# A three-pass fp32 trunk on one core: half changes that keep the last pair's weights, first residuals in a pool of their own, casts queued behind a copy, and the final norm's loads one step ahead

## The chip, the cores and the metric

One of the eight cores of a Trainium2 chip runs the whole program: TensorE (PE) multiplies, VectorE (DVE) and ScalarE (ACT) do everything elementwise, SyncE (SP) issues the loads and stores. The time is the device time of one execution in microseconds, given as the median of the runs shown.

## What is computed

The reference is one layer of a trunk on x of shape (1, 2048, 1024) in float32, cut here to what matters:

```python
h = rmsnorm(x, norm_mix_w)
proj = jnp.einsum("btd,dc->btc", h, w_in)            # 5648 columns
u_b, u_c, u_h, z, xbc, dt_raw = jnp.split(proj, SPLITS, axis=-1)
y_a = u_b * causal_dwconv(u_c * u_h, conv_w)         # gated short convolution
y_b = ssd_mixer(z, xbc, dt_raw, ...)                 # Mamba-2 scan in chunks of 64, 16 heads
x = x + jnp.einsum("btc,cd->btd", jnp.concatenate([y_a, y_b], axis=-1), w_out)
h = rmsnorm(x, norm_mlp_w)
hid = jnp.square(jax.nn.relu(jnp.einsum("btd,df->btf", h, w_up)))   # 4096 wide
x = x + jnp.einsum("btf,fd->btd", hid, w_down)
return rmsnorm(x, final_norm_w)
```

## The kernel before

**Products.** Every float32 operand is split into a high part (a cast, made on ScalarE: `L103` for weights, `L319` for activations) and a low part (operand minus high part, a subtraction on VectorE: `L104` and `L320`). A product is three matmuls, high by high (`L269`), high by low (`L270`), low by high (`L271`). The input projection, the MLP's up projection and its down projection use a Strassen-like scheme with seven products in place of eight (`Seven.chain`): for a pair of weight blocks and two blocks of 512 positions come the products b11, t1, t2, b21, t3, b22 and t4 in this order, each 12 matmuls of 128x512 (four pieces of the depth times three), 84 matmuls in all. They use PSUM accumulators that the profile calls px, py and pw. Behind b11 ScalarE copies px to pw (`L277`), and t2 adds on to px only when that copy has read it. Behind each other product ScalarE or VectorE takes the accumulator out (`evict`), and the next product that uses its bank waits for that.

**Halves.** The 2048 positions are two halves, each two blocks of 512. Weight pairs are the outer work, activations of one half stay in the core's memory (tiles uh and ul: seven combinations of blocks for each piece of the depth, kept in four groups, 0 to 3, of two, two, two and one). While the seven products of a pair run, a generator `ahead` makes the next pair's weights: two loads (wraw), four sums (`combine`), four casts, four subtractions. In the first half of the input projection (`first_half`, pairs in the order of `PAIRS`) the sums are stored to HBM (`sums_d`) and the second half (`second_half`, order `LATER`) loads them back. In the last pair of a half, `refresh` or, ahead of the down projection, `refill` loads the next stage's activations (rb from hm_d or hn_d, rh from hid_d; a ring of four buffers uraw) and splits them by `settle`, group by group as products finish with the old ones: group 0 is loaded behind b11 and split behind t1, group 1 behind t1 and b21, group 2 behind b21 and b22, group 3 behind b22 and t4.

**Beside the pairs.** `prepare` makes the norm and the combinations of the second half's activations from x in many small steps; in the first half of the projection one step follows each product, in the MLP one follows b11, t2 and t3. `dt_part` makes the time steps of the scan, at its end with two small matmuls (`L640`) that use what VectorE computed just before.

**The MLP.** `pair` takes each result through relu and square (`L860`, `L861`); two results are a copy of one accumulator (`L854`) plus another (`L857`). `store` combines them and stores them to hid_d.

**The down projection.** `STEPS` is a table of steps. An entry (h, d, fs) is a group: half h, output block d, hidden pieces fs; a step is one run of the seven products over all its groups' pieces. `REFILL` says which hidden group is loaded and split beside a step. A tile acc for each quarter of an output holds the residual x1_d, loaded by `outs` ahead of the step, and `L986` adds the accumulators to it on VectorE. When the first half's outputs are done, `finish_first` makes their final norm beside the remaining steps: it loads lf from fin_d, squares and sums it, takes the root, and a reciprocal of 128x512 on VectorE (`L171`), then loads again, scales (`L1124`) and stores.

**What orders the work.** Every engine works through its own queue in order. A scheduler sets that order from the order in which the code is written and the engines' loads; `reuse_waits="tile"` pools and semaphores say what waits. So a waiting instruction holds all that stands behind it on its engine.

## Time and profile before

| what | value |
| --- | --- |
| median of 3 runs (lowest, highest) | 2642.49 us (2636.65, 2643.14) |
| profiled execution, its time | 2640.53 us |
| its span from first to last instruction | 2638.8 us |
| TensorE's mean granted clock | 0.998 |
| DMA moved | 511.25 MB, 194 GB/s |

A row of a timeline reads: start, length, engine, line, operation, output <- input, shapes, count, and in brackets the idle time ahead of it with what ended it. Times are microseconds from the span's start. A row of a group ends with busy time and mean ns of one instruction, then the idle time ahead of the group and its releaser. TensorE's matmuls overlap, so a matmul's length (0.39 us) is more than its distance to the next (0.23 us). `PE px L269 <- ACT pw L277` is: the matmul of line 269 into px waited for line 277 on ScalarE, the copy into pw.

### The profile page before, as it was taken

How to read it: one execution, taken by the hardware profiler on the slowest of the kernel's cores; microseconds unless marked ns; L12 is line 12 of the kernel's file. 1: busy time of each engine (PE TensorE's matmuls, PEld its weight loads, DVE VectorE, ACT ScalarE, POOL GpSimd, SP SyncE). 2: the span in 40 equal slices, each digit the busy share in tenths (PEclk: the TensorE clock that was granted, in tenths of full speed). 3: DMA queues.
4: the chain of work that ended last, by engine and by line, in shares of the span. 5: the costliest groups of instructions: out<-in, count | busy, mean ns of one | idle time of the engine just before them, and what ended most of it. 6: DMA issues, size and time to landing. Idle time of an engine off the chain costs nothing.

```text
span 2638.8 us, 33504 instructions
## 1 busy us (share of the span) xinstructions
PE 2588.8 (98%) x12034; PEld 2127.0 (81%) x12034; DVE 1955.7 (74%) x2696; ACT 1432.9 (54%) x2175; POOL 58.2 (2%) x98
## 2 busy tenths in 40 slices
PE   7999999999999999999999999999999999999998
PEld 5778888788888888888888888788887888888777
DVE  7987676777777777778767765755558877888885
ACT  6644345777667666666326555655555444444443
POOL 0000010000000000000000000000000000000001
PEclk9999999999999999999999999999999999999999
DMA  3585344655555578977665674744448554665762
GB/s 146 190 302 191 137 151 168 207 162 163 171 160 183 154 253 266 283 221 224 211 210 211 232 271 140 261 158 140 161 148 294 165 150 150 214 210 180 238 202 72
DMA packets 283718, 511.25 MB, mean 194 GB/s; under 512 B 25248, under 2 KB 139936, under 8 KB 283552
## 3 DMA queue, kind: packets, MB, share of 16 engines
q1 hardware_dynamic: 283552, 509.12, 58.6%
q8 instruction: 94, 1.54, 0.2%
q14 instruction: 72, 0.59, 0.1%
HBM read 343.88 MB, written 165.15 MB: 193 GB/s over the span
## 4 chain that ended last, share of the span: by engine, by line
PE 65%; issue 25%; DMA 4%; DVE 3%; ACT 3%; SPq 0%; POOL 0%; POOLq 0%; DVEq 0%; ACTq 0%
PE px L269 9%; PE px L271 9%; PE px L270 9%; PE py L269 5%; PE py L271 4%; PE py L270 4%; PE pm L112 4%; PE pm L113 4%; PE pm L114 4%; PE pw L269 2%; PE pw L271 2%; PE pw L270 2%; DMA dec<-rd_d 1%; PE yd L1280 1%; PE yo L1277 1%
## 5 line engine op out<-in xcount | busy, mean ns | idle before, releaser
L269 PE MATMUL px<-uh,whi 128*128 128x512 f32 x1672 | 656.9, 393 | 10.3 <-ACT pw L277 5.6
L271 PE MATMUL px<-uh,wlo 128*128 128x512 f32 x1672 | 651.4, 390 | 2.6 <-DVE wlo L104 2.6
L270 PE MATMUL px<-ul,whi 128*128 128x512 f32 x1672 | 651.9, 390 | 0.0
L269 PEld LDWEIGHTS px<-uh,whi 128*128 128x128 f32 x1672 | 314.1, 188 | 84.7 <-ACT pw L277 8.1
L104 DVE TENSOR_TENSOR wlo<-wraw,whi 128x1024 fp32r<-128x1024 f32 x230 | 233.2, 1014 | 197.9 <-ACT whi L103 197.8
L271 PEld LDWEIGHTS px<-uh,wlo 128*128 128x128 f32 x1672 | 314.3, 188 | 69.5 <-DVE wlo L104 3.4
L270 PEld LDWEIGHTS px<-ul,whi 128*128 128x128 f32 x1672 | 314.4, 188 | 63.8
L103 ACT CAST whi<-wraw 128x1024 fp32r<-128x1024 f32 x230 | 203.5, 885 | 283.3 <-PE px L270 192.1
L103 ACT CAST whi<-s 128x1024 fp32r<-128x1024 f32 x210 | 219.6, 1046 | 233.1 <-PE py L270 76.1
L269 PE MATMUL py<-uh,whi 128*128 128x512 f32 x836 | 326.9, 391 | 2.3 <-DVE acc L986 1.9
L270 PE MATMUL py<-ul,whi 128*128 128x512 f32 x836 | 325.5, 389 | 0.0
L271 PE MATMUL py<-uh,wlo 128*128 128x512 f32 x836 | 325.3, 389 | 0.0
L104 DVE TENSOR_TENSOR wlo<-s,whi 128x1024 fp32r<-128x1024 f32 x210 | 255.2, 1215 | 88.9 <-ACT whi L103 87.0
L112 PE MATMUL pm<-uh,whi 128*128 128x512 f32 (+1 forms) x648 | 252.0, 390 | 2.1 <-ACT uh L204 2.1
L114 PE MATMUL pm<-uh,wlo 128*128 128x512 f32 (+1 forms) x648 | 248.3, 383 | 0.0
L113 PE MATMUL pm<-ul,whi 128*128 128x512 f32 (+1 forms) x648 | 248.3, 383 | 0.0
L269 PEld LDWEIGHTS py<-uh,whi 128*128 128x128 f32 x836 | 156.9, 188 | 35.9 <-DVE acc L986 2.3
L271 PEld LDWEIGHTS py<-uh,wlo 128*128 128x128 f32 x836 | 156.9, 188 | 32.8
L270 PEld LDWEIGHTS py<-ul,whi 128*128 128x128 f32 x836 | 157.0, 188 | 32.2
L269 PE MATMUL pw<-uh,whi 128*128 128x512 f32 x418 | 163.4, 391 | 0.7 <-ACT pw L277 0.7
L319 ACT CAST uh<-rh 128x1024 fp32r<-128x1024 f32 (+1 forms) x128 | 120.4, 944 | 79.1 <-PE py L271 64.4
L271 PE MATMUL pw<-uh,wlo 128*128 128x512 f32 x418 | 162.9, 390 | 0.0
(233 smaller groups left out, 3750.3 us busy)
## 6 DMA issues: line engine op xcount, KB each, us to landing
hid_d<-e SPq DMA_DIRECT2D x96, 512.0 KB, 3.9
rh<-hid_d SPq DMA_DIRECT2D x96, 512.0 KB, 4.4
wraw<-w_in SPq DMA_DIRECT2D x68, 512.0 KB, 4.2
wraw<-w_up SPq DMA_DIRECT2D x64, 512.0 KB, 4.3
wraw<-w_down SPq DMA_DIRECT2D x104, 256.0 KB, 3.7
dec<-rd_d SPq DMA_DIRECT2D x32, 512.0 KB, 5.7
wraw<-w_out SPq DMA_DIRECT2D x32, 512.0 KB, 5.1
x_d<-xt SPq DMA_DIRECT2D x64, 256.0 KB, 3.9
```

The source lines that it names most:

```text
L103: nc.scalar.copy(hi, raw)
L104: eng.tensor_tensor(out=lo, in0=raw, in1=hi.bitcast(F32), op=ALU.subtract)
L112: nc.tensor.matmul(out, whi, hi, start=(k == 0), stop=False)
L113: nc.tensor.matmul(out, whi, lo, start=False, stop=False)
L114: nc.tensor.matmul(out, wlo, hi, start=False, stop=(k == nk - 1))
L269: nc.tensor.matmul(p, hi, h[0], start=bool(first and k == 0), stop=False, **kw)
L270: nc.tensor.matmul(p, hi, h[1], start=False, stop=False, **kw)
L271: nc.tensor.matmul(p, lo, h[0], start=False, stop=(k == len(g) - 1), **kw)
L319: nc.scalar.copy(p[i][0], t)
L1277: nc.tensor.matmul(yo[:, j * L : (j + 1) * L], state[:, j * P : (j + 1) * P], cT, start=True, stop=True)
L1280: nc.tensor.matmul(yd[(i % 2) * 64 : (i % 2) * 64 + 64, (i // 2) * L : (i // 2 + 1) * L], byhead(t["xdt"])[:, i, :], t["dec"][:, i, :], st ...
```

## The change

- The second halves begin with the pair whose weights the first half ended with (`LATER` starts with z6, z0 goes next to last; in the MLP piece 15 comes first), so the last pair of a first half makes no weights ahead. z0's sums are made anew in the second half.
- In `refresh` and `refill` the casts of a group are queued behind the copy of b11 (`issue_after`): groups 0 to 2 behind this pair's copy, group 3 behind the next pair's.
- `prepare` beside the projection's first half goes on three times a pair in place of seven. `dt_part` of the second half waits two steps more ahead of its small matmuls.
- The down projection starts with two steps of two groups; step 0 has no residuals: ScalarE copies its first eight results into tiles of a pool `ap`, which isn't memory of the MLP. Their residuals are loaded (rx, in the ring uraw) and added by VectorE beside steps 3 and 4. Two hidden groups are loaded and split in the MLP's last pair in place of four; the others beside steps 0 and 1. The last pair's results are stored to hid_d behind those loads' code.
- The reciprocal of 128x512 is two of 128x256. `finish_first` loads one step ahead.

The diff, with little of the unchanged text around it:

```diff
 import itertools
-from contextlib import ExitStack
+from contextlib import ExitStack, nullcontext
...
             nc.scalar.activation(rb, ps_, AF.Sqrt, bias=eps, scale=self.scale)
-            nc.vector.reciprocal(out=rb, in_=rb)
+            for h in (slice(0, w // 2), slice(w // 2, w)):
+                nc.vector.reciprocal(out=rb[:, h], in_=rb[:, h])
             return rb
...
             self.places = [{} for _ in range(4)]
+            self.unsettled = None
...
                         pm[gi]["w"] = psum("mw", "pw", accs["mw"])
-                        nc.scalar.copy(pm[gi]["w"], pm[gi]["x"])
+                        self.copied = nc.scalar.copy(pm[gi]["w"], pm[gi]["x"]).ins
                     else:
                         evict(name, gi, pm[gi])
+                if name == "b11" and self.unsettled:
+                    self.settle(*self.unsettled, self.copied)
+                    self.unsettled = None
                 if ahead is not None:
...
-        def settle(self, places, i, got):
+        def settle(self, places, i, got, after=None):
             for p, t in zip(places, got):
                 p[i] = self.place(i)
-                nc.scalar.copy(p[i][0], t)
+                with tc.issue_after(after) if after is not None else nullcontext():
+                    nc.scalar.copy(p[i][0], t)
                 nc.vector.tensor_tensor(out=p[i][1], in0=t, in1=p[i][0].bitcast(F32), op=ALU.subtract)
...
             i = {"t1": 0, "b21": 1, "b22": 2, "t4": 3}.get(name)
-            if i is not None:
-                self.settle(self.new, i, self.got)
+            if i == 3:
+                self.unsettled = self.new, i, self.got
+            elif i is not None:
+                self.settle(self.new, i, self.got, self.copied)
             i = {"b11": 0, "t1": 1, "b21": 2, "b22": 3}.get(name)
...
         PAIRS = "ch0 ch1 b0 x0 x8 ch2 ch3 b2 x2 ch4 ch5 b4 x4 x10 ch6 ch7 b6 x6 z4 z6".split()
-        LATER = "z0 x0 z4 ch0 ch1 b0 x8 ch2 ch3 b2 x2 ch4 ch5 b4 x4 x10 ch6 ch7 b6 x6 z6 z2".split()
+        LATER = "z6 x0 z4 ch0 ch1 b0 x8 ch2 ch3 b2 x2 ch4 ch5 b4 x4 x10 ch6 ch7 b6 x6 z0 z2".split()
         FIRST = {"z": 24, "x": 32, "b": 0}
...
             )
-            yield
-            yield
-            yield
+            for _ in range(3 + 2 * self.h):
+                yield
             pc = psum("tp", "pc", 2)
...
             if h == 0:
-                sums_d[what] = dram.tile([P, 2, 1024], F32, name=f"sums_{what}_d")
+                if what != self.LATER[0]:
+                    sums_d[what] = dram.tile([P, 2, 1024], F32, name=f"sums_{what}_d")
                 raws = self.load_cols(w_in, self.cols(what))()
                 yield
-                yield from self.combine(*raws, sums_d[what])
+                yield from self.combine(*raws, sums_d.get(what))
                 return
...
                         pass
-                    ahead = self.weights(1, self.LATER[0])
+                    ahead = None
                     self.new = [{} for _ in range(4)]
...
                 def after(name):
-                    next(late, None)
+                    if name in ("b11", "t2", "t3"):
+                        next(late, None)
                     if last:
...
-                ws = self.pair(0, what, ws, ahead, after)
+                ws = self.pair(0, what, ws, ahead, after) or ws
             self.places = self.new
...
         def tmp(self, name):
-            return self.up.tile([P, TB], F32, tag="utmp", name=name, bufs=8)
+            return self.up.tile([P, TB], F32, tag="utmp", name=name, bufs=self.tmps)
...
             got = self.chain([self.places], ws, ahead, evict, after)
-            self.store(h, q, e0, e1, e2)
+            self.unstored = h, q, e0, e1, e2
             return got
...
         def half(self, h, ws, late):
-            for q in range(NQ):
-                last = q + 1 == NQ
+            order = list(range(NQ))
+            if h == 1:
+                order = order[-1:] + order[:-1]
+            for m, q in enumerate(order):
+                last = m + 1 == NQ
                 if not last:
-                    ahead = self.weights(self.load_cols(w_up, (2 * q + 2, 2 * q + 3)))
+                    n = 2 * order[m + 1]
+                    ahead = self.weights(self.load_cols(w_up, (n, n + 1)))
                 elif h == 0:
...
                         pass
-                    ahead = self.weights(self.load_cols(w_up, (0, 1)))
+                    ahead = None
                 else:
...
                     else:
-                        self.refill((0, 1, 2, 3), name)
+                        self.refill((0, 1), name)
-                ws = self.pair(h, q, ws, ahead, after)
+                ws = self.pair(h, q, ws, ahead, after) or ws
+                if h == 1 and last:
+                    self.refill((REFILL[0],), "b11")
+                self.store(*self.unstored)
             if h == 0:
...
             if i is not None:
-                self.settle([self.wides.setdefault(g, {}) for g in gs], i, self.got)
+                todo = [self.wides.setdefault(g, {}) for g in gs], i, self.got
+                if i == 3 and len(gs) > 1:
+                    self.unsettled = todo
+                else:
+                    self.settle(*todo, self.copied)
             i = {"b11": 0, "t1": 1, "b21": 2, "b22": 3}.get(name)
...
+        QUARTERS = (("c11", 0, 0), ("c22", 4, 1), ("c12", 0, 1), ("c21", 4, 0))
+        AHEAD = ("c22", "c12", "c11")
+        FREE = {(0, 0): AHEAD, (0, 2): AHEAD, (1, 1): AHEAD[:2], (1, 2): AHEAD[:1], (1, 3): AHEAD}
+        def places_for(self, h, d):
+            t = self.acc[h, d] = {}
+            for n, _, _ in self.QUARTERS:
+                free = n in self.FREE.get((h, d), ())
+                pool, bufs = (self.ap, 6) if free else (self.dp, 12)
+                t[n] = pool.tile([P, TB], F32, tag="acc", name="acc", bufs=bufs)
         def outs(self, h, d):
-            t = {}
-            for n, i, bb in (("c11", 0, 0), ("c22", 4, 1), ("c12", 0, 1), ("c21", 4, 0)):
-                t[n] = self.dp.tile([P, TB], F32, tag="acc", name="acc", bufs=18)
-                nc.sync.dma_start(t[n], x1_d[h * NBB + bb][:, d + i])
-            self.acc[h, d] = t
+            self.places_for(h, d)
+            for n, i, bb in self.QUARTERS:
+                nc.sync.dma_start(self.acc[h, d][n], x1_d[h * NBB + bb][:, d + i])
+        def residual(self, d):
+            ts = []
+            for bb in range(NBB):
+                t = self.raw("rx")
+                nc.sync.dma_start(t, x1_d[bb][:, d : d + 5 : 4])
+                ts.append(t)
+            yield
+            for n, i, bb in self.QUARTERS:
+                o = self.acc[0, d][n]
+                nc.vector.tensor_tensor(out=o, in0=o, in1=ts[bb][:, i // 4], op=ALU.add)
+                if n == "c22":
+                    yield
+            yield
...
             for d in range(4):
-                self.outs(0, d)
+                if d % 2:
+                    self.outs(0, d)
+                else:
+                    self.places_for(0, d)
             late = None
+            RESIDUAL = {3: 0, 4: 2}
             for n, step in enumerate(STEPS):
...
                     late = self.finish_first()
+                elif n in RESIDUAL:
+                    late = self.residual(RESIDUAL[n])
...
                     t = self.acc[h, d][c]
-                    nc.vector.tensor_tensor(out=t, in0=pm[p], in1=t, op=ALU.add)
+                    if n == 0 and name not in ("t3", "b22"):
+                        nc.scalar.copy(t, pm[p])
+                    else:
+                        nc.vector.tensor_tensor(out=t, in0=pm[p], in1=t, op=ALU.add)
                     if fin:
...
                     g = REFILL.get(n)
-                    if g is not None:
+                    if g is not None and (n or name != "b11"):
                         self.refill((g,), name)
...
                 acc = self.dp.tile([P, TB], F32, tag="facc", name="facc", bufs=1)
+                ahead = load(0)
+                yield
                 for d in range(0, KD, 2):
-                    t = load(d)
+                    t, ahead = ahead, load(d + 2) if d + 2 < KD else None
                     nc.scalar.activation(t, t, AF.Square)
...
                 r = st.whole(acc)
+                ahead = load(0)
                 yield
                 for d in range(0, KD, 2):
-                    t = load(d)
+                    t, ahead = ahead, load(d + 2) if d + 2 < KD else None
                     for i in range(2):
...
-    STEPS = [[(0, 0, [0, 1, 2, 3])], [(0, 2, [0, 1])], [(0, 1, [0]), (0, 3, [0, 1, 2])]]
-    REFILL = {2: 4}
+    STEPS = [[(0, 0, [0, 1]), (0, 2, [0, 1])], [(0, 1, [0]), (0, 3, [0, 1, 2])], [(0, 0, [2, 3])]]
+    REFILL = {0: 2, 1: 3, 2: 4}
     for n in range(1, 2 * NQ - 3):
...
     mlp.wides = {}
+    mlp.tmps = 8
     with tc.tile_pool(name="up", bufs=1, reuse_waits="tile") as mlp.up:
         ws = mlp.half(0, ws, mlp.prepare(1, x1_d, C_NMLP))
+    mlp.ap = c4.enter_context(tc.tile_pool(name="ap", bufs=1, reuse_waits="tile"))
+    mlp.tmps = 4
+    with tc.tile_pool(name="up1", bufs=1, reuse_waits="tile") as mlp.up:
         ws = mlp.half(1, ws, iter(()))
```

The first place is ScalarE at the MLP's change of halves, around the copy of the next pair's b11 (pw <- px). The casts uh <- rb are the new half's activations, whi <- are weights, e the MLP's results. Before:

```order
L319 CAST uh_14363<-rb 128x1024
L319 CAST uh_14367<-rb 128x1024
L861 ACTIVATE e_14191<-e_14191 128x512
L103 CAST whi<-wraw 128x512
L319 CAST uh_14371<-rb 128x1024
L319 CAST uh_14401<-rb 128x512
L277 COPY pw<-px 128x512
L319 CAST uh_14405<-rb 128x512
L319 CAST uh_14409<-rb 128x512
L103 CAST whi<-wraw 128x1024
```

Now:

```order
L325 CAST uh_14320<-rb 128x1024
L870 ACTIVATE e_14169<-e_14169 128x512
L325 CAST uh_14324<-rb 128x1024
L869 ACTIVATE e_14170<-px 128x512
L325 CAST uh_14328<-rb 128x1024
L870 ACTIVATE e_14170<-e_14170 128x512
L279 COPY pw<-px 128x512
L325 CAST uh_14388<-rb 128x512
L325 CAST uh_14392<-rb 128x512
L325 CAST uh_14396<-rb 128x512
```

The casts of weights are gone from in front of the copy, and the four of group 3 (128x512) stand behind it. The four of group 2 (128x1024) stand in front of it as they did.

The second place is VectorE in the pair just before, from the first subtractions ul <- rb on. The additions e <- px and e <- py empty the accumulators for t4 of this pair and for the next pair. Before:

```order
L320 TENSOR_TENSOR ul_14248<-rb,uh_14247 128x1024
L104 TENSOR_TENSOR wlo<-wraw,whi 128x1024
L320 TENSOR_TENSOR ul_14299<-rb,uh_14298 128x1024
L104 TENSOR_TENSOR wlo<-s_14291,whi 128x1024
L857 TENSOR_TENSOR e_14192<-px,s_14229 128x512
L320 TENSOR_TENSOR ul_14303<-rb,uh_14302 128x1024
L320 TENSOR_TENSOR ul_14307<-rb,uh_14306 128x1024
L320 TENSOR_TENSOR ul_14311<-rb,uh_14310 128x1024
L857 TENSOR_TENSOR e_14190<-py,s_14271 128x512
```

Now:

```order
L326 TENSOR_TENSOR ul_14223<-rb,uh_14222 128x1024
L326 TENSOR_TENSOR ul_14263<-rb,uh_14262 128x1024
L326 TENSOR_TENSOR ul_14267<-rb,uh_14266 128x1024
L326 TENSOR_TENSOR ul_14271<-rb,uh_14270 128x1024
L866 TENSOR_TENSOR e_14171<-px,s_14208 128x512
L326 TENSOR_TENSOR ul_14275<-rb,uh_14274 128x1024
L866 TENSOR_TENSOR e_14169<-py,s_14246 128x512
```

Three subtractions of group 1 stand now between the end of group 0 and the addition e <- px, where one and two of the weights' subtractions stood; the last one comes behind that addition.

The third place is ScalarE at the start of the down projection: the last results of the MLP, and then step 0. Here uh <- rh are the hidden tiles, and acc <- the results of step 0. Before:

```order
L319 CAST uh_16703<-rh 128x1024
L861 ACTIVATE e_16528<-e_16528 128x512
L319 CAST uh_16707<-rh 128x1024
L860 ACTIVATE e_16529<-px 128x512
L319 CAST uh_16711<-rh 128x1024
L861 ACTIVATE e_16529<-e_16529 128x512
L103 CAST whi<-wraw 128x512
L319 CAST uh_16741<-rh 128x512
L277 COPY pw<-px 128x512
L319 CAST uh_16745<-rh 128x512
L319 CAST uh_16749<-rh 128x512
L103 CAST whi<-wraw 128x512
```

Now:

```order
L103 CAST whi<-s_16628 128x1024
L870 ACTIVATE e_16488<-e_16488 128x512
L869 ACTIVATE e_16489<-px 128x512
L103 CAST whi<-wraw 128x512
L870 ACTIVATE e_16489<-e_16489 128x512
L279 COPY pw<-px 128x512 x2
L325 CAST uh_16723<-rh 128x512
L325 CAST uh_16727<-rh 128x512
L1039 COPY acc<-py 128x512
L325 CAST uh_16757<-rh 128x1024
L1039 COPY acc<-py 128x512
L325 CAST uh_16802<-rh 128x1024
```

The copies pw <- px stand ahead of the casts of group 3, of which two are left there, and the copies into acc are new on ScalarE.

2 lines of the change are left out of this document (1 added, 1 removed).

## The prediction

> **What bounds the kernel now.** I read the page's first part first, then the chain of waits (the waits of TensorE, grouped by what ended them), then TensorE's busy time by stretch, and the timelines of the places that these two name. The profiled execution took 2640.53 us with a span of 2638.8; the three timed runs had a median of 2642.49 (2636.65 to 2643.14), so the profiled one lies 2 us under the median.
>
> The page's busy shares:
>
> ```profile
> PE 2588.8 (98%) x12034; PEld 2127.0 (81%) x12034; DVE 1955.7 (74%) x2696; ACT 1432.9 (54%) x2175; POOL 58.2 (2%) x98
> ```
>
> TensorE is the bound: 2638.8 - 2588.8 = 50 us of the span are not its own. The change leaves its matmuls as they are (no product is added or taken away), so it can only give back waits. These are the waits of TensorE at the start and then those that lie in the stages touched (engine and line, waited-for engine and line, total, times, longest):
>
> ```profile
> PE pst L131 <- DVE facc L469: 12.9, 1, 12.9
> PE px L269 <- ACT pw L277: 5.6, 4, 2.5
> PE px L271 <- DVE wlo L104: 2.6, 2, 1.5
> PE px L269 <- DVE acc L986: 2.5, 5, 0.8
> PE py L269 <- DVE acc L986: 1.9, 1, 1.9
> PE px L269 <- ACT s L705: 1.3, 1, 1.3
> ```
>
> The first, at the start, is not touched. The others make 13.9 us, some 0.5% of the time: that sets the scale. TensorE by stretch of 66 us (from : to, length, busy, instructions, granted clock, DMA share, GB/s) shows where they lie:
>
> ```profile
> 132.00:198.00 66.00, 62.36 (x271) 1.00 0.83 302
> 198.00:264.00 66.00, 65.74 (x290) 1.00 0.54 192
> 264.00:330.00 66.00, 66.00 (x293) 1.00 0.39 137
> 1650.00:1716.00 66.00, 63.54 (x273) 0.97 0.75 266
> 1980.00:2046.00 66.00, 61.75 (x272) 1.00 0.86 293
> ```
>
> A stretch without waits holds 293 matmuls, 0.225 us each. What a disturbed stretch lost is its missing matmuls times that: 22 x 0.225 = 5.0 us in 132 to 198 (first half of the input projection), 4.5 in 1650 to 1716 (the MLP's change of halves), 4.7 in 1980 to 2046 (start of the down projection).
>
> **The change of halves in the MLP.** TensorE there:
>
> ```profile
> 1692.18 0.39 PE L270 MATMUL py<-ul,whi 128*128 128x512 f32 x1
> 1692.41 0.39 PE L271 MATMUL py<-uh,wlo 128*128 128x512 f32 x1
> 1695.26 0.50 PE L269 MATMUL px<-uh,whi 128*128 128x512 f32 x1 [2.46 <-ACT pw L277]
> ...
> 1699.72 0.40 PE L269 MATMUL pw<-uh,whi 128*128 128x512 f32 x1
> ```
>
> From 1692.41 to 1695.26 is 2.85 us where a matmul's pitch is 0.23, so 2.62 are lost (a wait shown as w costs about w + 0.16, since the ends of matmuls are modelled). The twelve matmuls from 1695.26 to 1699.72 then took 4.46 us instead of 12 x 0.225 = 2.70: another 1.76, and the stretch's clock fell to 0.97. In all 4.4 us. The Trainium skill (page "TensorE: Matmul & The Clock Gate", Part 1) says the clock is halved after an idle window of about 3.4 us. By this rule a wait of 2.46 us would not do it, the 1.76 us would be no price of this wait, and the sum below would be 1.8 us smaller; the rows show the slow matmuls right behind a shorter wait, and I go by the rows.
>
> ScalarE ahead of the copy that TensorE waits for, VectorE in the product before, and the issue of the loads that feed those casts:
>
> ```profile
> 1692.94 1.78 ACT L319 CAST uh<-rb 128x1024 fp32r<-128x1024 f32 x2
> 1694.63 0.58 ACT L277 COPY pw<-px 128x512 f32<-128x512 f32 x1
> ```
>
> ```profile
> 1680.79 1.22 DVE L320 TENSOR_TENSOR ul<-rb,uh 128x1024 fp32r<-128x1024 f32 x1 [2.18 <-ACT uh L319]
> ...
> 1683.36 0.68 DVE L857 TENSOR_TENSOR e<-px,s 128x512 f32<-128x512 f32 x1
> 1683.96 3.49 DVE L320 TENSOR_TENSOR ul<-rb,uh 128x1024 fp32r<-128x1024 f32 x3
> ```
>
> ```profile
> rb<-hn_d SPq DMA_DIRECT2D x16, 512.0 KB, 5.6
> ```
>
> ```profile
> 1684.47 0.39 PE L269 MATMUL px<-uh,whi 128*128 128x512 f32 x1
> ```
>
> The change takes the next weights' four casts, four subtractions and four sums out of this pair, and the last group of casts goes behind the copy. It does not take the third group of casts from in front of it, and these wait for loads whose buffers come free only as the second group's subtractions end. In the new order three of those subtractions stand ahead of the addition now at 1683.36, against one now: 1680.79 + 3 x 1.16 (3.49 / 3) = 1684.3 for the addition, done at 1685.0, so t4, at 1684.47 now, starts some 0.5 to 1 us late. The fourth subtraction ends near 1686.1; its buffer's load lands 5.6 us later at 1691.7; the cast (0.95) and one square (0.5) behind it put the copy at 1693.2, and t2 at about 1693.9, where without waits it would start at 1692.64. So 1.2 to 1.9 us stay and the half clock goes: of 4.4 I take 2.7 back (bounds 0, if the load comes no earlier than now, and 4.4).
>
> **The start of the down projection.** TensorE, and VectorE ahead of the second wait:
>
> ```profile
> 2004.20 0.50 PE L269 MATMUL px<-uh,whi 128*128 128x512 f32 x1 [2.39 <-ACT pw L277]
> ...
> 2017.24 0.50 PE L269 MATMUL py<-uh,whi 128*128 128x512 f32 x1 [1.86 <-DVE acc L986]
> ```
>
> ```profile
> 2015.56 0.69 DVE L986 TENSOR_TENSOR acc<-pw,acc 128x512 f32<-128x512 f32 x1 [0.38 <-DMA acc<-x_d]
> ```
>
> 2.55 and 2.02, together 4.6. The first wait is the same copy behind the same kind of casts (sixteen hidden tiles there; the change loads half as many in the last pair, and the rest from steps 0 and 1 on). The second is a residual that comes late, since its buffer is memory of the MLP that must be stored first. In the new order step 0 needs no residual and no buffer of that memory: ScalarE copies into a pool of its own. No copy stands behind an unfinished load there. I take 4.4 back (bounds 1, if the hidden tiles still come late, and 4.6).
>
> The work goes elsewhere, on VectorE. Durations of a split's subtraction in its two sizes, of an accumulation, and VectorE's stretch that begins in step 0 and holds most of steps 1 to 4:
>
> ```profile
> L320 DVE TENSOR_TENSOR ul<-rh,uh 128x1024 fp32r<-128x1024 f32 x96 | 116.5, 1219 | 23.1 <-ACT uh L319 22.9
> ...
> L986 DVE TENSOR_TENSOR acc<-px,acc 128x512 f32<-128x512 f32 x105 | 71.4, 685 | 41.6 <-PE px L271 41.4
> ...
> L320 DVE TENSOR_TENSOR ul<-rh,uh 128x512 fp32r<-128x512 f32 x32 | 21.8, 683 | 0.2 <-ACT uh L319 0.2
> ```
>
> ```profile
> 2016.00:2082.00 66.00, 55.38 (x74) 1.00 0.68 222
> ```
>
> Two hidden groups move in here, each 3 x 1.22 + 0.68 = 4.3 us, 8.7 in all. Eight residual additions are new, 8 x 0.685 = 5.5. Accumulations, six to a group, were 24 in the first three steps (four groups) and are 30 (five), of which 8 are ScalarE's: two fewer, -1.4. That is 12.8 us more over five steps, against a slack of 66 - 55.4 = 10.6 in the stretch and what step 0 leaves idle. VectorE gets full for three or four steps, but its weights are due only a step later: cost 1 us (bounds 0 and 3).
>
> **The input projection.** TensorE in the first half, then at the change of halves:
>
> ```profile
> 175.21 0.50 PE L271 MATMUL px<-uh,wlo 128*128 128x512 f32 x1 [1.49 <-DVE wlo L104]
> ...
> 191.09 0.50 PE L271 MATMUL px<-uh,wlo 128*128 128x512 f32 x1 [1.08 <-DVE wlo L104]
> ```
>
> ```profile
> 464.27 0.50 PE L269 MATMUL px<-uh,whi 128*128 128x512 f32 x1 [0.50 <-DVE eb L708]
> 478.32 0.50 PE L269 MATMUL px<-uh,whi 128*128 128x512 f32 x1 [1.29 <-ACT s L705]
> ...
> 506.88 0.43 PE L640 MATMUL pc<-dts,tri 128*128 128x64 f32 x2 [0.44 <-DVE dts L633]
> ```
>
> In the first half the norm's steps for the other half run beside the pairs, seven a pair, and VectorE is late with weights. Three a pair spread them over more than twice the pairs. The stretches 132 to 264 lost 25 matmuls, 5.6 us; the same VectorE work remains and some pairs with convolutions are full by themselves, so I take 4.0 back (bounds 2 and 5.6). At the change of halves 0.66 + 1.45 + 0.6 = 2.7, and as an estimate another 0.6 like the last row for the second block's chain: 3.3, of which the removed load of weights, the later casts and the two more steps of delay for the chain should leave about 1: 2.3 back (bounds 1 and 3.3). For that, the weights of z0 have no stored sums and are summed anew in the second half, beside a pair full of convolutions. The row of such an addition:
>
> ```profile
> L208 DVE TENSOR_TENSOR s<-wraw 128x512 f32<-128x512 f32 x84 | 57.4, 684 | 0.3
> ```
>
> Four of them, 2.7 us of VectorE: cost 0 to 2, I take 0.7, since one pair in front it has slack.
>
> **The first norm of the output**, in the last quarter of the down projection. VectorE's waits there, and the reciprocal:
>
> ```profile
> DVE lf L1124 <- DMA lf<-fin_d: 3.3, 3, 1.7
> ```
>
> ```profile
> L171 DVE RECIPROCAL facc<-facc 128x512 f32<-128x512 f32 x8 | 26.8, 3346 | 1.4 <-ACT facc L170 1.4
> ```
>
> VectorE works in order, so accumulations behind the waiting or the 3.3-us instruction come late: the five waits "px <- acc L986" above, 2.5 + 5 x 0.16 = 3.3 us. Loads one step ahead end the first kind; the reciprocal in two halves lets an accumulation in between, if the scheduler puts one there. The halves stand next to each other in the new order, so that part gives nothing. 2.0 back (bounds 0 and 3.3). The loads ahead hold two of the four buffers that the hidden tiles use as well.
>
> **Sum.** 2.7 + 4.4 - 1.0 + 4.0 + 2.3 - 0.7 + 2.0 = 13.7 us. 2640.5 - 13.7 = 2626.8, about 2627. All terms at their good ends: 4.4 + 4.6 + 5.6 + 3.3 + 3.3 = 21.2, 2619. All at their bad ends: 0 + 1 - 3 + 2 + 1 - 2 + 0 = -1, 2641.5. A measurement of this kernel tells about 0.3% from no change, 7.9 us: below 2634.6 counts as faster, above 2650.4 as slower (from the median of 2642.5).
>
> **The rivals.** *The waits are only handed on.* In-order queues keep the same casts; the copy still stands behind a cast that waits for a load. For it: the third group in the MLP, above. Against it: in two of four places the work itself leaves the pair. Then the down projection gives 2, the first half 2, the rest 1: 5 us, 2635.5, which counts as the same. Chance 0.22.
>
> *VectorE's slack was more than enough and every wait goes:* 2619. For it: an addition of 0.69 us rarely hits a due weight. Against it: the three subtractions in front of t4. Chance 0.13.
>
> *The hidden tiles come late in steps 0 to 4 of the down projection, and it gets slower.* The residuals of these steps are loaded through the four buffers that the hidden tiles use, and are freed only when a full VectorE has added them:
>
> ```profile
> rh<-hid_d SPq DMA_DIRECT2D x96, 512.0 KB, 4.4
> ```
>
> A cast that waits for such a load holds ScalarE's queue, and the copy behind it holds TensorE. A load issued when its cast is due costs 4.4 us and one issue, some 5; with that in each of five steps 25 us, against 13.7 + 1.0 gained: 2650.8 or more. It decides from 3 us a step on. Against it: hidden tiles of a step are due a step later. Chance 0.08.
>
> **How the numbers follow.** The forecast has 0.57; it and the full gain (0.13) lie under 2634.6: faster 0.70. The handing-on rival counts as the same: 0.22. Slower 0.08. The range goes from 2617 (the full gain, and 2 us for the spread of the runs) to 2641 (the bad ends of all terms).
>
> **What would show it.** In the profile after: no wait on the copy at the start of the down projection and none on accumulations there; at the MLP's change of halves a wait on the copy of 1 to 2 us with no slow matmuls behind it; no "px <- wlo" waits of over a microsecond in the first half; no VectorE wait on lf. Wrong it is if the start of the down projection has its waits again, now on ScalarE's copies, or if steps 1 to 4 show waits on accumulations that add up to over 5 us.

## The result and the profile after

The changed kernel took 2625.68 us in the median (2618.76 to 2629.97, 6 runs), the kernel before 2640.95 us (2636.65 to 2643.14, 6 runs): a ratio of 0.9942, with a 95% interval of 0.9932 to 0.9952. The profiled execution took 2625.95 us, 14.6 less than that of before; the forecast sum was 13.7. The page's busy shares:

```profile
PE 2585.2 (99%) x12034; PEld 2127.5 (81%) x12034; DVE 1948.6 (74%) x2698; ACT 1433.1 (55%) x2177; POOL 56.7 (2%) x98
```

The waits of TensorE after the change, those of the stages touched (lines are those of the new kernel: `L271` was `L269`, `L279` was `L277`, `L1041` was `L986`):

```profile
PE px L271 <- DVE acc L1041: 4.2, 4, 2.7
...
PE px L271 <- ACT s L712: 0.9, 1, 0.9
PE px L271 <- DVE e L866: 0.5, 1, 0.5
...
PE px L271 <- ACT pw L279: 0.2, 1, 0.2
```

The waits on wlo and on py's accumulation are gone, those on the copy fell from 5.6 to 0.2 us. One line grew: the waits of px on accumulations, from 2.5 to 4.2. TensorE by stretch, the later ones moved by the 9 us and more that the kernel had then gained:

```profile
132.00:198.00 66.00, 66.00 (x293) 1.00 0.50 180
198.00:264.00 66.00, 65.92 (x291) 1.00 0.74 264
1641.00:1707.00 66.00, 65.43 (x287) 1.00 0.72 255
1971.00:2037.00 66.00, 66.00 (x292) 1.00 0.77 257
```

To compare stages I add up, over the 128x512 matmuls of a stage, how far the start of the next instruction lies beyond 0.2267 us, the pitch without waits (differences under 0.03 left out). Lost time of TensorE in us, from one profile of each kernel; the columns are the projection's first half from 66 us on, its change of halves (446 to 594), the MLP's (1640 to 1716), steps 0 to 4 of the down projection (1970 to 2112), the stretch of the first half's final norm (2376 to 2600), and the whole:

| kernel | first half | change, projection | change, MLP | down, steps 0-4 | final norm | whole |
| --- | --- | --- | --- | --- | --- | --- |
| before | 7.4 | 5.7 | 4.3 | 4.8 | 4.0 | 50.3 |
| changed | 1.7 | 4.0 | 1.1 | 0.2 | 5.7 | 34.6 |
| changed, second profile (e11) | 1.0 | 3.9 | 1.0 | 1.5 | 6.9 | 40.6 |
| no look-ahead (e1) | 1.1 | 3.7 | 1.4 | 0.1 | 7.6 | 39.9 |
| norm's cast later (e2) | 1.8 | 3.9 | 0.3 | 2.2 | 5.4 | 37.0 |
| casts in front (e3) | 1.5 | 4.0 | 2.6 | 1.4 | 3.7 | 30.9 |
| norm every product (e4) | 6.1 | 2.8 | 1.1 | 0.8 | 4.8 | 36.9 |
| residuals first (e5) | 1.1 | 3.4 | 0.9 | 8.8 | 2.9 | 35.6 |
| weights made again (e6) | 1.2 | 5.6 | 4.9 | 0.9 | 4.4 | 37.5 |
| sum behind addition (e7) | 1.2 | 3.7 | 0.6 | 0.2 | 2.4 | 28.3 |
| and whole reciprocal (e8) | 1.1 | 3.0 | 1.2 | 1.0 | 1.7 | 30.4 |
| and split behind addition (e9) | 0.9 | 3.7 | 1.2 | 1.2 | 2.8 | 28.8 |
| and in the MLP (e10) | 1.8 | 3.7 | 3.9 | 0.5 | 1.6 | 29.9 |

Behind some waits TensorE ran at half clock for a while; that is in these numbers, with about 1.5 us each at the MLP's change in before, e6 and e10, in the final norm of e1 and e11, and about 1.0 in the down projection of e5 (the last section tells when it comes). How far chance goes is seen where the code is the same: the output projection and the scan between 960 and 1280 us lost 6.6 to 12.0 us in these profiles, and the two profiles of the changed kernel differ by 6.0 in the whole. Differences of under 1.5 us at one place are not read.

**The MLP's change of halves.** TensorE, VectorE and ScalarE of the changed kernel, at the places that the prediction worked out:

```profile
1676.57 0.50 PE L271 MATMUL px<-uh,whi 128*128 128x512 f32 x1 [0.49 <-DVE e L866]
```

```profile
1673.55 2.36 DVE L326 TENSOR_TENSOR ul<-rb,uh 128x1024 fp32r<-128x1024 f32 x2 [0.87 <-ACT uh L325]
1675.83 0.68 DVE L866 TENSOR_TENSOR e<-px,s 128x512 f32<-128x512 f32 x1
```

```profile
1682.59 1.03 ACT L325 CAST uh<-rb 128x1024 fp32r<-128x1024 f32 x1
1683.52 0.63 ACT L870 ACTIVATE e<-e 128x512 f32<-128x512 f32 x1
1684.06 0.58 ACT L279 COPY pw<-px 128x512 f32<-128x512 f32 x1
1684.57 1.13 ACT L325 CAST uh<-rb 128x512 fp32r<-128x512 f32 x2
```

TensorE waits 0.49 us (0.65 lost) for the addition behind three subtractions. The copy comes at 1684.06; the third group is still in front of it, the last group behind it. TensorE loses another 0.24 there, and no slow matmuls follow. The chain to the copy is the forecast one: the fourth subtraction of the second group (1676.43) ends at 1677.65, the load into the buffer that it frees goes out at 1677.67 and lands at 1682.26, and the cast that waits for it starts at 1682.59.

**Where it got worse: the final norm.** TensorE and VectorE of the changed kernel at its longest wait, and SyncE's own waits around it:

```profile
2490.50 0.39 PE L273 MATMUL py<-uh,wlo 128*128 128x512 f32 x1
2493.56 0.50 PE L271 MATMUL px<-uh,whi 128*128 128x512 f32 x1 [2.67 <-DVE acc L1041]
```

```profile
2487.84 1.21 DVE L104 TENSOR_TENSOR wlo<-s,whi 128x1024 fp32r<-128x1024 f32 x1
2492.21 0.69 DVE L233 TENSOR_TENSOR s<-wraw 128x512 f32<-128x512 f32 x1 [3.15 <-DMA wraw<-w_down]
2492.82 0.68 DVE L1041 TENSOR_TENSOR acc<-px,acc 128x512 f32<-128x512 f32 x1
```

```profile
SPq L940 <- DVE wlo L104: 8.3, 2, 6.5
```

VectorE has no wait on lf any more (3.3 us before, over the stretch). It is held for 3.15 us by the first sum of the next weights, which waits for a load of w_down, and the accumulation that TensorE needs stands behind it. The load went out late: SyncE waited up to 6.5 us for the subtraction that frees its buffer. ScalarE's waits on the hidden tiles in this stretch grew from 6.5 to 21.3 us. The same sum held an accumulation in the kernel before, too, though for less time; this is VectorE there:

```profile
2506.29 0.69 DVE L231 TENSOR_TENSOR s<-wraw 128x512 f32<-128x512 f32 x1 [2.58 <-DMA wraw<-w_down]
2506.90 0.68 DVE L986 TENSOR_TENSOR acc<-px,acc 128x512 f32<-128x512 f32 x1
```

Of the five accumulations that TensorE waited for before, two stood right behind, or one instruction behind, a wait on lf (0.66 and 0.60 us lost); the others stood behind this sum (0.51), behind two sums of the norm (0.95) and in a full queue (0.55). None stood behind a reciprocal.

### The profile page after: what moved, and what is told of

Same layout as the page of the kernel before. It is cut to its first block, busy times and chain, and to the rows that moved or that the text cites. A ratio compares the mean times of both kernels' runs of the same rounds, so it can differ in the third digit from the quotient of the medians.

```text
span 2624.1 us, 33507 instructions
## 1 busy us (share of the span) xinstructions
PE 2585.2 (99%) x12034; PEld 2127.5 (81%) x12034; DVE 1948.6 (74%) x2698; ACT 1433.1 (55%) x2177; POOL 56.7 (2%) x98
## 4 chain that ended last, share of the span: by engine, by line
PE 62%; issue 25%; DMA 4%; DVE 4%; ACT 3%; SPq 0%; POOL 0%; POOLq 0%; DVEq 0%; ACTq 0%
PE px L271 9%; PE px L273 9%; PE px L272 9%; PE py L271 4%; PE py L272 4%; PE py L273 4%; PE pm L112 4%; PE pm L113 4%; PE pm L114 4%; PE pw L271 2%; PE pw L272 2%; PE pw L273 2%; DMA dec<-rd_d 2%; PE yd L1338 1%; PE yo L1335 1%
## 5 line engine op out<-in xcount | busy, mean ns | idle before, releaser
L271 PE MATMUL px<-uh,whi 128*128 128x512 f32 x1672 | 655.9, 392 | 6.0 <-DVE acc L1041 4.2
L271 PEld LDWEIGHTS px<-uh,whi 128*128 128x128 f32 x1672 | 313.9, 188 | 79.4 <-DVE acc L1041 8.6
L104 DVE TENSOR_TENSOR wlo<-wraw,whi 128x512 fp32r<-128x512 f32 (+2 forms) x227 | 230.1, 1014 | 186.5 <-ACT whi L103 186.2
L103 ACT CAST whi<-wraw 128x512 fp32r<-128x512 f32 (+2 forms) x227 | 200.9, 885 | 272.8 <-PE px L272 189.5
L103 ACT CAST whi<-s 128x1024 fp32r<-128x1024 f32 (+1 forms) x206 | 215.5, 1046 | 232.1 <-PE py L272 98.5
L271 PE MATMUL py<-uh,whi 128*128 128x512 f32 x836 | 326.8, 391 | 0.0
L104 DVE TENSOR_TENSOR wlo<-s,whi 128x1024 fp32r<-128x1024 f32 (+1 forms) x206 | 250.2, 1215 | 81.1 <-ACT whi L103 79.8
L271 PEld LDWEIGHTS py<-uh,whi 128*128 128x128 f32 x836 | 157.0, 188 | 32.9 <-issue 0.5
L271 PE MATMUL pw<-uh,whi 128*128 128x512 f32 x418 | 163.2, 391 | 0.0
```

The costliest lines, as they stand in the source:

```text
L103: nc.scalar.copy(hi, raw)
L104: eng.tensor_tensor(out=lo, in0=raw, in1=hi.bitcast(F32), op=ALU.subtract)
L271: nc.tensor.matmul(p, hi, h[0], start=bool(first and k == 0), stop=False, **kw)
```

## The experiments

Each is the changed kernel with the edit shown, and timed against the kernel before; the time is the median, the ratio has its 95% interval. Runs of one group (e1 to e4, e5 to e8, e9 to e11) shared a chip.

### e1: no look-ahead in the final norm

```diff
-                ahead = load(0)
-                yield
                 for d in range(0, KD, 2):
-                    t, ahead = ahead, load(d + 2) if d + 2 < KD else None
+                    t = load(d)
```

and the same in the loop that scales and stores.

> The changed kernel, but the final norm of the first half loads its tiles when they are due, as before (the reciprocal stays in two halves). In the changed kernel the stretch of that norm lost 5.5 us of TensorE in waits on accumulations and on one copy (0.69, 0.32, 0.72, 2.83 and small ones), against 4.0 before. Theory: the tiles loaded ahead hold two of the ring's four buffers, so hidden tiles' loads, and behind them on SyncE the weights' loads, come late; without the look-ahead ScalarE's waits on rh fall from 19.5 to under 10 us, VectorE's waits on lf come back (some 3 us), the wait of 2.7 us is gone, and the time is the changed kernel's or up to 2 us less. Rival: the look-ahead is sound and the 2.7 us have another cause (the norm's cast behind the sums): then the lf waits come on top, and the time is 2 to 4 us more.

2625.27 us, 0.9941 (0.9925 to 0.9957). The longest wait of TensorE in the stretch, what VectorE waits for just ahead of it, and ScalarE's waits on lf:

```profile
2472.14 0.50 PE L271 MATMUL px<-uh,whi 128*128 128x512 f32 x1 [3.21 <-DVE acc L1041]
```

```profile
2469.58 0.69 DVE L1168 TENSOR_TENSOR facc<-facc,lf 128x512 f32<-128x512 f32 x1 [2.07 <-ACT lf L1163]
...
2471.40 0.69 DVE L1041 TENSOR_TENSOR acc<-px,acc 128x512 f32<-128x512 f32 x1
```

```profile
ACT lf L1163 <- DMA lf<-fin_d: 21.4, 6, 5.7
```

Both halves come out in part. ScalarE's waits on rh fall to 5.9 us, as the theory of the ring has it, and the wait at 2490 is gone. But its waits on lf rise from 13.2 to 21.4, VectorE's sums wait for them, and another accumulation is held, at 2472. The stretch loses 7.6 against 5.7 and 6.9 (with half clock left out, some 6.0 against 5.7 and 5.5): no gain. The load that is late is another one; the accumulation behind it is late either way.

### e2: the norm's cast one step later

```diff
+                yield
                 st = self.rstd()
                 st.parts(acc)
```

> The changed kernel, with one more step between the last sum of the final norm and the cast that needs it (ahi). In the changed kernel ScalarE waited 3.36 us on that cast, the next weights' cast behind it came late, so its buffer and the load into it, and TensorE waited 2.7 us. Theory of the cast: this wait goes, 2 to 3 us less time than the changed kernel's. Rival (the ring of buffers is at fault): a wait of over 1 us on an accumulation stays within 15 us of that place, and the time moves by under 1.5 us.

2623.96 us, 0.9928 (0.9912 to 0.9943). VectorE at the same place:

```profile
2493.55 0.69 DVE L233 TENSOR_TENSOR s<-wraw 128x512 f32<-128x512 f32 x1 [3.19 <-DMA wraw<-w_down]
2494.16 0.69 DVE L1041 TENSOR_TENSOR acc<-px,acc 128x512 f32<-128x512 f32 x1
```

ScalarE has no wait on the norm's cast there any more (3.36 us in the changed kernel), and the same sum waits 3.19 us for the same load. The theory of the cast falls; the stretch loses 5.4. The ratio is lower, but the trace shows nothing gained at this place, and the interval overlaps that of the changed kernel.

### e3: the casts where the code has them

```diff
-                with tc.issue_after(after) if after is not None else nullcontext():
-                    nc.scalar.copy(p[i][0], t)
+                nc.scalar.copy(p[i][0], t)
...
-            if i == 3:
-                self.unsettled = self.new, i, self.got
-            elif i is not None:
-                self.settle(self.new, i, self.got, self.copied)
+            if i is not None:
+                self.settle(self.new, i, self.got)
```

> The changed kernel, with the casts of refresh and refill where the code has them, not behind the copy of b11; the weights of the last pair are still kept. Theory: the order on the queue is what ended the wait on the copy; with the casts of the last group (they wait for loads that land up to 6 us after the copy is due) in front again, TensorE waits on the copy 1.5 to 3 us at each of three places (both changes of halves, start of the down projection), in all 3 to 8 us more time. Rival: taking the weights' casts out was enough; under 1 us of waits on the copy, time within 1.5 us of the changed kernel's.

2625.43 us, 0.9939 (0.9923 to 0.9955). ScalarE at the MLP's change of halves:

```profile
1677.95 0.61 ACT L324 CAST uh<-rb 128x512 fp32r<-128x512 f32 x1
1678.73 0.62 ACT L324 CAST uh<-rb 128x512 fp32r<-128x512 f32 x1 [0.17 <-DMA rb<-hn_d]
1679.26 0.58 ACT L279 COPY pw<-px 128x512 f32<-128x512 f32 x1
```

Two casts of the last group stand in front of the copy again; TensorE waits 1.01 us for it, 1.17 lost, where the changed kernel lost 0.24 to this copy and its second profile nothing. The place as a whole loses 2.6 in place of 1.1; the rest of that is a wait on the addition (1.16), which costs 0 to 1.3 us in the profiles that have the changed order. At the start of the down projection 1.4 in place of 0.2 is within chance, at the projection's change nothing moves. So the order on the queue is worth about 1 us at one place, by one profile. That is far from the 3 to 8 of the theory and close to the rival's "under 1 us of waits", and the time, within 0.3 us of the changed kernel's, doesn't show it.

### e4: the norm behind every product

```diff
-                    if name in ("b11", "t2", "t3"):
-                        next(late, None)
+                    next(late, None)
```

> The changed kernel, with the norm of the second half going on behind each of the seven products of a pair in the projection's first half, as before. Theory: VectorE gets late with weights again in the first pairs; waits on wlo of over 1 us come back near 175 and 190 us, TensorE's loss between 66 and 264 us goes from 1.7 back to 6 to 7.5 us, and the time is 4 to 6 us more. Rival: the loss there moved to later pairs, so the time changes by under 2 us.

2630.11 us, 0.9956 (0.9942 to 0.9969). TensorE:

```profile
175.26 0.50 PE L273 MATMUL px<-uh,wlo 128*128 128x512 f32 x1 [1.50 <-DVE wlo L104]
...
190.84 0.50 PE L273 MATMUL px<-uh,wlo 128*128 128x512 f32 x1 [0.76 <-DVE wlo L104]
```

The waits of before are back at their places, the first half loses 6.1 in place of 1.7, and the time is 4.4 us over the changed kernel's 2625.68, and 4.7 to 6.2 over that of e1 to e3 on the same chip, which have the changed kernel's first half. The term is shown, in the trace and in the time.

### e5: residuals first, one pool

```diff
-        FREE = {(0, 0): AHEAD, (0, 2): AHEAD, (1, 1): AHEAD[:2], (1, 2): AHEAD[:1], (1, 3): AHEAD}
+        FREE = {}
...
-                if d % 2:
-                    self.outs(0, d)
-                else:
-                    self.places_for(0, d)
+                self.outs(0, d)
...
-            RESIDUAL = {3: 0, 4: 2}
+            RESIDUAL = {}
```

with `acc` in one pool of 18, and VectorE's addition in step 0 too.

> The changed kernel, but step 0 of the down projection has its residuals loaded ahead and VectorE adds to them, in one pool of 18 tiles, as before; the order of the steps and the casts' places stay as changed. Theory: the second wait of before comes back (TensorE waits 1.5 to 2.5 us in step 0 on an accumulation that waits for a residual's load); the copy stays unhindered; time 1.5 to 3 us more than the changed kernel's. Rival: the earlier stores of the MLP's results (its tiles are stored some 4 us sooner in the changed order) already bring the loads in time; no wait over 0.5 us in step 0, time within 1 us, and VectorE has eight additions less to do in steps 3 and 4.

2627.45 us, 0.9958 (0.9945 to 0.9971). TensorE, and SyncE's issue of the loads:

```profile
1995.70 0.79 PE L271 MATMUL py<-uh,whi 128*128 128x512 f32 x1 [6.55 <-DVE acc L1038]
```

```profile
1984.19 2.36 SPq L853 DMA_DIRECT2D hid_d<-e  x2
1986.65 0.38 SPq L854 DMA_DIRECT2D hid_d<-t  x1
1987.12 1.42 SPq L961 DMA_DIRECT2D rh<-hid_d  x2
1988.59 7.33 SPq L981 DMA_DIRECT2D acc<-x_d  x11
```

The wait is 6.55 us, not 1.5 to 2.5: the residuals' loads go out from 1988.59 on, behind the MLP's last stores and hidden tiles' loads, and the accumulation that empties py starts at 1994.95, when the residual that it needs has landed (1994.93). Matmuls at half clock follow. The place loses 8.8 in place of 0.2; the rival, that the sooner stores suffice, falls. The time is only 1.8 us more, since this profile lost less at the scan and the norm; that part is chance or the eight additions less, which isn't told apart.

### e6: the next half's weights made again

```diff
-    LATER = "z6 x0 z4 ch0 ch1 b0 x8 ch2 ch3 b2 x2 ch4 ch5 b4 x4 x10 ch6 ch7 b6 x6 z0 z2".split()
+    LATER = "z0 x0 z4 ch0 ch1 b0 x8 ch2 ch3 b2 x2 ch4 ch5 b4 x4 x10 ch6 ch7 b6 x6 z6 z2".split()
...
-                    ahead = None
+                    ahead = self.weights(1, self.LATER[0])
```

and the same in the MLP.

> The changed kernel, but the last pairs of the first halves make the next weights again (order of the pairs as before), while the casts of activations stay queued behind the copy. Theory: the weights' work is half of the cause: at the MLP's change of halves TensorE loses 2 to 4 us (changed: 1.1) and at the projection's 0.5 to 2 more than the changed kernel's 3.9; the time is 2 to 4 us more. Rival: the queue order alone does it; under 0.7 us more at both places together.

2628.19 us, 0.9953 (0.9941 to 0.9965). ScalarE and TensorE at the MLP's change of halves:

```profile
1683.35 0.60 ACT L103 CAST whi<-wraw 128x512 fp32r<-128x512 f32 x1
1683.86 1.04 ACT L325 CAST uh<-rb 128x1024 fp32r<-128x1024 f32 x1
1684.81 0.57 ACT L279 COPY pw<-px 128x512 f32<-128x512 f32 x1
```

```profile
1685.43 0.50 PE L271 MATMUL px<-uh,whi 128*128 128x512 f32 x1 [2.34 <-ACT pw L279]
```

With the weights' work back, queueing the last group behind the copy does not help: 4.9 us lost, as before (4.3), some 1.5 of either at half clock. What TensorE lost to the copy alone, without the half clock, makes a table of four: neither 2.62, the queue alone (e6) 2.51, the weights alone (e3) 1.17, both 0.24 and, in the second profile, nothing. So the weights' work is the larger part of this wait, and the order takes what is left once it is gone; the first three rest on one profile each. At the projection's change 5.6 us are lost, where the profiles with kept weights lost 2.8 to 4.0. The time is 2.5 us more than the changed kernel's, with intervals that overlap.

### e7: the next weights' sum behind the addition

```diff
-            nc.vector.tensor_tensor(out=s12[:, a], in0=r1[:, a], in1=r1[:, b], op=ALU.add)
+            with tc.issue_after(self.added) if self.added is not None else nullcontext():
+                nc.vector.tensor_tensor(out=s12[:, a], in0=r1[:, a], in1=r1[:, b], op=ALU.add)
```

`added` is the accumulation of t3, beside the final norm only, and the sum is made behind t3, not behind b21.

> The changed kernel, but beside the final norm of the first half the first sum of the next weights (it waits for the load of w_down) stands on VectorE behind the accumulation of t3, not ahead of it. Theory: the wait of 2.7 us at 2490 is VectorE held by that sum, up to 3.2 us, with the due accumulation behind it; it goes, the stretch of the norm loses under 2.5 us in place of 5.5, and the time is 2 to 4 us less than the changed kernel's, a ratio near 0.993. Rival: the weights are the true limit; then TensorE waits on wlo or whi of that pair instead, by 1.5 us or more, and the time stays.

2621.16 us, 0.9925 (0.9913 to 0.9937). TensorE's one wait on an accumulation in the stretch, and VectorE at the old place:

```profile
PE px L275 <- DVE acc L1046: 1.9, 1, 1.9
```

```profile
2483.38 0.69 DVE L1046 TENSOR_TENSOR acc<-px,acc 128x512 f32<-128x512 f32 x1 [0.71 <-PE px L277]
2483.99 0.68 DVE L237 TENSOR_TENSOR s<-wraw 128x512 f32<-128x512 f32 x1
```

The accumulation goes first, now VectorE waits for TensorE there, and the sum behind it finds its load landed. The stretch loses 2.4, and TensorE doesn't wait on the weights: the rival falls. One profile would be little, but e8 to e10 keep this order, and the four lose 2.4, 1.7, 2.8 and 1.6, against 2.9 to 6.9 in the six with the norm as changed (see e11). The ratios of e7 to e9 (0.9922 to 0.9928) lie below the changed kernel's 0.9942, some 4 us; each interval alone still overlaps or touches that one.

### e8: the reciprocal whole again

```diff
-            for h in (slice(0, w // 2), slice(w // 2, w)):
-                nc.vector.reciprocal(out=rb[:, h], in_=rb[:, h])
+            nc.vector.reciprocal(out=rb, in_=rb)
```

on top of e7.

> As the kernel with the sum behind the addition, and the reciprocal of 128x512 in one instruction of 3.3 us as before. Theory: the two halves stand next to each other, so nothing changes: the same waits to 0.5 us near the reciprocal (2485 and 2400). Rival: an accumulation is served between the halves or sooner; then a wait of 0.5 to 1.5 us on an accumulation comes back right behind the reciprocal.

2619.48 us, 0.9922 (0.9909 to 0.9935). TensorE has no wait near either reciprocal; the halves give nothing. The wait that is left lies at 2463; ScalarE and VectorE ahead of it:

```profile
2461.83 1.05 ACT L328 CAST uh<-rh 128x1024 fp32r<-128x1024 f32 x1 [4.23 <-DMA rh<-hid_d]
```

```profile
2462.91 1.23 DVE L329 TENSOR_TENSOR ul<-rh,uh 128x1024 fp32r<-128x1024 f32 x1 [2.65 <-ACT uh L328]
2464.05 0.68 DVE L1045 TENSOR_TENSOR acc<-px,acc 128x512 f32<-128x512 f32 x1
```

Here a hidden tile is late: ScalarE waits 4.23 us for its load, the subtraction waits for the cast, and the accumulation stands behind the subtraction. The load went out at 2455.92, after SyncE had waited 1.2 us for a store of lf, whose buffer is of the same ring. This is the fastest version, 0.8% under the kernel before.

### e9 and e10: the hidden tiles' subtraction behind the addition too

```diff
     class Mlp(Seven):
+        SETTLE = {"t1": 0, "t3": 1, "b22": 2, "t4": 3}
+        FETCH = {"b11": 0, "t1": 1, "t3": 2, "b22": 3}
...
-            i = {"t1": 0, "b21": 1, "b22": 2, "t4": 3}.get(name)
+            i = self.SETTLE.get(name)
...
-            i = {"b11": 0, "t1": 1, "b21": 2, "b22": 3}.get(name)
+            i = self.FETCH.get(name)
...
-                nc.vector.tensor_tensor(out=p[i][1], in0=t, in1=p[i][0].bitcast(F32), op=ALU.subtract)
+                with tc.issue_after(first) if first is not None else nullcontext():
+                    nc.vector.tensor_tensor(out=p[i][1], in0=t, in1=p[i][0].bitcast(F32), op=ALU.subtract)
```

on top of e8: group 1 is split, and group 2 loaded, behind t3 in place of b21, and `first` is t3's addition. e9 has this in `refill`, e10 in `refresh` of the MLP as well.

> As the kernel with the sum behind the addition and the whole reciprocal, and in the refill of the down projection the second group of a hidden tile is split behind the accumulation of t3 as well (its subtraction stood ahead of that accumulation and waited, through its cast, for a load of rh). Theory: the wait of 1.3 to 1.9 us on an accumulation near 2460 was that subtraction; it goes, and the stretch of the norm loses under 1.2 us; time 1 to 2 us less, near 2619, ratio 0.9915 to 0.992. Rival: the hidden tiles are late altogether, so TensorE waits on ul or uh of the next step instead, or the wait moves to the accumulation of b22; no gain.

> As the kernel with the split behind the addition, and at the MLP's change of halves group 1 is split behind the addition of t3 too. Theory: the wait on that addition (0.5 to 1.1 us there) goes, but the third group's loads come some 1.7 us later, since their buffers come free later, and the casts in front of the copy with them: TensorE waits on the copy 0.5 to 2 us; the place loses 1 to 2.5 us in place of 0.6 to 1.3. Rival: the loads land early enough; the place loses under 0.4 us.

e9: 2620.69 us, 0.9928 (0.9915 to 0.9942); e10: 2623.62 us, 0.9937 (0.9925 to 0.995). In e9 the single wait gives way to three of up to 0.5 us:

```profile
PE px L277 <- DVE acc L1056: 1.4, 3, 0.5
```

The stretch loses 2.8 (and 1.6 in e10, with the same code there) against 1.7 in e8, so the 1.2 us expected are not reached and nothing is gained. In e10, TensorE at the MLP's change of halves:

```profile
1683.14 0.79 PE L277 MATMUL px<-uh,whi 128*128 128x512 f32 x1 [2.08 <-ACT pw L285]
```

TensorE no longer waits for the addition of t3, but for the copy, 2.24 us lost, and half clock follows: 3.9 us in place of 1.2. The theory had 1 to 2.5, without the clock. Set against e9 at the same matmul, the third group's loads land 1.4 to 2.2 us later and the copy starts 1.3 us later, as the theory has it.

### e11: the changed kernel again

> The changed kernel itself, timed beside the other two on one chip: ratio to before 0.993 to 0.9955. If the stretch of the norm loses 1.5 us more or less than the 5.7 of its first profile, that much of it is chance (arrival of loads), not order.

2624.22 us, 0.9942 (0.993 to 0.9955). The final norm's stretch lost 6.9 here. The six profiles with the norm as changed (the two, e3 to e6) lost 5.7, 6.9, 3.7, 4.8, 2.9 and 4.4, 4.7 in the mean, against 4.0 in the one profile of before: the look-ahead and the split gave nothing that can be read. (e3 has the hidden tiles' casts in another order; without it the mean is 4.9.)

## Why the prediction was right, and where it was not

The time, its sign and its size were right: 2625.68 against 2627, and 14.6 us between the profiles against 13.7. So was the mechanism, that only TensorE's waits can be given back: its matmuls are as many as before, and its lost time fell by 15.7 (9.7 by the second profile). The terms behind the sum were not all right, and that it came out within 1 us is in part luck: the first half and the start of the down projection gave more than forecast, z0's sums cost nothing, and this made up for the final norm, which gave nothing.

- **The MLP's change of halves**: 2.7 forecast, 4.3 - 1.1 = 3.2 measured. The addition behind three subtractions cost TensorE 0.65 (0.5 to 1 forecast). The copy was forecast at 1693.2, that is 1684.2 in the new kernel, whose matmuls come there 9.0 us sooner; it came at 1684.06. The remaining loss was put at 1.2 to 1.9 and was 0.9, and the wait on the copy that was to be seen, 1 to 2 us, was 0.2. Some 1.5 of the 3.2 are the half clock behind the wait of before, which another execution of that kernel need not have had (last section). By e3 and e6 the weights' work is the larger part of what had to go.
- **The start of the down projection**: 4.4 less 1.0 for a full VectorE, 3.4 forecast, 4.8 - 0.2 = 4.6 measured. VectorE did get full in steps 1 to 4, 61.07 us of 66 where it had 55.38:

```profile
2004.00:2070.00 66.00, 61.07 (x85) 1.00 0.70 228
```

  and TensorE lost 0.2 there. The cost of 1.0 was too much for this profile, but the eight with these steps as changed (the two, e1, e2, e4 and e6 to e8) lost 0.1 to 2.2, 0.9 in the mean, so it was about right. The hidden tiles did not hold up steps 0 to 4, so the slower rival had no case. What the own pool avoids was put at 2.0, and e5 lost 8.8 without it. The two numbers don't measure the same thing: in the changed order of steps TensorE needs the emptied py 24 matmuls (5.4 us) sooner than before, while the residuals' loads go out only some 9 matmuls (2 us) sooner.
- **The first half of the projection**: 4.0 forecast, 7.4 - 1.7 = 5.7 measured, of which 5.0 lie between 132 and 264 us, where the forecast counted; e4 gives 4.4 back in the trace and in the time. The step that failed was "some pairs with convolutions are full by themselves": they were not late.
- **The projection's change of halves**: 2.3 forecast, 1.7 measured. The copy s, behind a cast that waits for its load, still costs 0.86 us of waiting.
- **z0's sums made anew**: 0.7 of cost forecast. The second half lost 5.5 (594 to 960 us) as changed, and 5.5 in e6, which has z0's stored sums back: no cost. Before it lost 8.1. Some 1.8 us of the fall are two waits of a scan matmul (pss) on ScalarE's xtok, at 597 and 769 us, which the changed kernel does not have; why they went no experiment tells. That gain stood in no term.
- **The final norm**: 2.0 back was forecast, nothing came, and in the first profile it lost 1.7 more. The step that failed was "loads one step ahead end the first kind". They did end VectorE's waits on lf, but of the 3.3 us counted only 1.26 stood right or one instruction behind such a wait, none behind a reciprocal, and the sum did not ask what is late next on the same queue: the next weights' sum (e7) and the hidden tiles' subtraction (e8) stand ahead of the due accumulations just as well. The rival of waits handed on was right at this one place of five.

Of the clock, the prediction took the rows against the rule of the Trainium skill (page "TensorE: Matmul & The Clock Gate", Part 1: a gate after an idle window of about 3.4 us). The experiments bear out that a shorter wait can be followed by half clock: 2.08 (e10), 2.34 (e6), 2.52 (e11). But the prediction counted the slow matmuls as a fixed price of this wait, and that they are not, see below.

## What to carry to other kernels

In the final norm late loads cost TensorE through what stood behind their readers on an in-order queue, so put the instruction that frees an accumulator ahead of the one that waits for a transfer: that took the stretch's loss from 4.7 us (mean of six profiles) to 2.1 (mean of e7 to e10), and loading sooner gave nothing that can be read. Where a queue is full around a change of stages, take work out first (keep weights that are loaded anyway) and order what is left second; the order alone gave nothing at the MLP's change (e6). When a wait is removed, follow the same queue to its next wait before counting the gain.

## What the runs showed of the hardware

Whether half clock follows a wait is not told by its length between 2 and 2.7 us. After idle times of 2.07 and 3.21 (e1), 2.08 (e10), 2.34 (e6), 2.46 (before), 2.52 (e11) and 6.55 (e5) the granted clock fell to a half, and 128x512 matmuls took 0.43 in place of 0.23 us each; some six to eight of them in most of these places, 1.2 to 1.8 us more. After 2.26 (e4), 2.39 (before), 2.45 and 2.61 (e2), 2.46 (e3), 2.61 (e8) and 2.67 (changed) it did not.

The traces do tell the two apart. Within a profile the granted clock changes only at moments that are whole multiples of 3.41 us apart. Cut into stretches at these moments, the wait of before lies in one stretch, and the longer one of the changed kernel is divided over two (from : to, length, busy, matmuls, granted clock):

```profile
1692.71:1696.12 3.41, 0.95 (x5) 1.00 0.88 290
1696.12:1699.53 3.41, 3.41 (x10) 0.50 0.96 360
```

```profile
2489.06:2492.47 3.41, 1.82 (x9) 1.00 0.46 165
2492.47:2495.88 3.41, 2.32 (x10) 1.00 0.00 0
2495.88:2499.30 3.42, 3.42 (x17) 1.00 0.71 188
```

In the thirteen profiles, between 30 and 2595 us, a stretch at half clock followed each full-clock stretch in which TensorE was idle for 2.04 us or more (seven of them, from 2.04 in e10 to 3.30 in e5), and none in which it was idle for 1.93 us or less (the most, in e8); none lies between. The moments stand at another place in each profile. So the same wait of 2 to 3 us has the price in one execution and not in the next, as the changed kernel's at 2490 shows: 2.67 us without it, 2.52 in the second profile with it.
